# Two matmuls for three in the split-precision products of a two-block network

## The chip, the cores and the metric

The kernel runs on one core of a Trainium2 chip. The time is that of one execution on the device in microseconds (us); of three runs the median is 3662.9 us, the lowest 3659.82 and the highest 3664.96.

## The reference

A sequence of 256 tokens of width 2048 goes through two blocks, in float32. What fills the time is matrix products of the 256 tokens with weights that are read once from memory.

```python
# block 1
mod = silu(c) @ w_ada + b_ada                        # 2048 x 12288, one row
h = modulate(rms_norm(x, norm1_w), shift1, scale1)
p = h @ w_in                                         # 2048 x 4112
x = x + gate1 * (concat(fourier_mix(..), mlstm(..)) @ w_out)      # 2048 x 2048
u = conv3(modulate(rms_norm(x, norm2_w), shift2, scale2) @ w_up)  # 2048 x 11264
a, v = split(u);  x = x + gate2 * ((silu(a) * v) @ w_down)        # 5632 x 2048
x = rms_norm(x, norm_f_w)
# block 2
h = x + 0.5 * rms_norm(swiglu(rms_norm(x)))          # gate and up 2048 x 5632 each, down 5632 x 2048
h = h + rms_norm(mix(rms_norm(h)))                   # S5 scan and sparse attention, ten projections
out = h + 0.5 * rms_norm(swiglu(rms_norm(h)))        # a second feed-forward layer of the same size
```

`mix` projects to the S5 input (1024 columns), keys and values (1536), queries (1024), gates (48), and two sigmoid gates (2048 each); then come a gated unit over the S5 output (1024 x 4096), the attention's output (1024 x 2048) and the last projection (2048 x 2048).

## The kernel before, in words

Everything is held feature-major: a tile has 128 features on the partitions and the 256 tokens along the free dimension (`P` = 128, `T` = 256). A product runs with the weight as the stationary operand, a 128 x 128 tile of it at a time, and the activation tile as the moving one, 256 columns.

Float32 precision comes from a split. Each weight chunk and each activation is written as a high and a low part, float32r tiles of 12 significant bits each, and three of the four cross products are summed: high weight with high activation, low weight with high activation, high weight with low activation. So one pair of a row tile k and a column tile (called a *tile product* below) costs three matmuls of 256 columns, each with a weight load of its own.

`STREAMS` (line 68) lists 21 weight streams with their row tiles and their groups of column tiles. `_tiles` and `_pairs` make groups of four column tiles; "qk_in" has one group of eight and "vg_in" one of four and a narrow one of 16 columns. `lin_steps` (line 317) walks a stream: for every group it takes PSUM banks, two column tiles to a bank, and for every chunk of 1024 weight columns per partition (two row tiles of a four-tile group, so eight tile products) calls `chunk`, then issues the matmuls: for each row tile k, four with the high weight, four with the low one, four with the high one again:

```python
for ci, (a, b) in enumerate(((hi, xh), (lo, xh), (hi, xl))):
    for j in js:
        self.mm(outs[j][0:widths[j]], a[:, c:c + widths[j]], b, ...)
```

`chunk` (line 305) starts the DMA of a raw chunk (SP's queue, four buffers `wr`), copies it to the high part `wh` on ACT (three buffers) and subtracts to get the low part `wl` (two buffers) on DVE, or on POOL for every `pool_every`-th chunk (every chunk of "qk_in" and "vg_in", each second one in the rest of block 1's first part and in the gated unit "glu2" and "gb_in2" of `mix2`, each fifth one at the head of `mix2`, none in the feed-forward layers).

When a group is complete, an evacuation function reads its banks. In the feed-forward layers `ev_up` multiplies or convolves the banks on DVE, applies Silu on ACT, multiplies on POOL and splits the result (`hidden`) into the `hh` and `hl` tiles. `ev_down` takes one column tile at a time, scales it on DVE and squares it on ACT for the next norm's statistics (`add_square`); a stream with `tile_evac` ends its last group tile by tile ("spread"), holding back the last two chunks. `post_norm` then makes the next stage's activations one row tile after the other: two multiplications and an addition on DVE and POOL, a high part on ACT, a low part on DVE.

Eight PSUM banks are one pool `ps` from which the groups and all small products draw. Work that is not on the streams runs as generators in the background: after each chunk `background` advances them by a set share of a step. In the first 500 us that is the modulation `ada_part` (100 MB of `w_ada`, summed on DVE) and the mLSTM and Fourier parts; in the feed-forward layer "up2" it is `s5_tables` (tables computed on POOL); in `mix2` it is the S5 scan (`s5`, on DVE and POOL) and the attention (`nsa`). The order on each engine is fixed when the program is built, by a planner that simulates a timeline (`schedule_with_timeline_sim=True`); a few stretches of DVE are ordered by hand (`manual_schedule` in `post_norm`). Tensors of one tag share a ring of buffers, and an instruction that takes a buffer waits for the last reader of the tile that was in it.

Of the kernel before, what the change touches and what calls it, by code (L numbers as in the profile page):

```python
# [14 lines left out]
P = 128  # L15
T = 256
# [8 lines left out]
# ---------------------------------------------------------------- host layout  # L25
# [6 lines left out]
# Heads are kept as (j, g): head g * 4 + j sits in column block j * 4 + g of the  # L32
# small per-head tables, and pair m holds heads of groups 2 * (m // 4) and the next.
# [18 lines left out]
# A stream is a list of groups; a group is a list of column tiles (index arrays).  # L52
def _tiles(cols, per=4, width=P):
    tiles = [cols[i:i + width] for i in range(0, len(cols), width)]
    return [tiles[i:i + per] for i in range(0, len(tiles), per)]


def _pairs(n_tiles, second):
    out = []
    for i in range(0, n_tiles, 2):  # L60
        out.append([_cols(i * P, P), _cols((i + 1) * P, P),
                    second + _cols(i * P, P), second + _cols((i + 1) * P, P)])
    return out
# [7 lines left out]
    "vg_in": ("w_in", 16, [_tiles(_cols(O_V, 512))[0] + [_cols(O_G, 16)]]),  # L71
# [22 lines left out]
def _chunks(kt, widths):  # L94
    """(first k-tile, k-tiles, offset) of every chunk of a group."""
# [16 lines left out]
def _fm(v):  # L112
    """[n * 128] -> [128, n]"""
    return np.ascontiguousarray(np.asarray(v).reshape(-1, P).T)
# [22 lines left out]
def _constants():  # L137
# [3 lines left out]
    dft = np.stack([c, s]).astype(np.float32)  # [2, 256, 256]  # L141
# [11 lines left out]
    # rows of the gates: forward heads on partitions 0-3, backward heads on 32-35  # L153
# [10 lines left out]
def prepare(inp):  # L164
# [13 lines left out]
    # shift and scale of the first norm, by pair of feature tiles: [pair, eighth of the rows, p, row tile, tile, 2, 128]  # L178
# [31 lines left out]
    for n in ("k", "v"):  # L210
        # rows of two neighbouring block positions fill the partitions: [chunk, (odd, d), pair, 256]
# [12 lines left out]
# ------------------------------------------------------------------- program  # L224


class Builder:
# [12 lines left out]
    # -- tiles  # L240
# [8 lines left out]
    def ring(self, dtype=F32):  # L249
        return self.new(self.p_ring, "r", [P, T], dtype)  # L250
# [7 lines left out]
    def ps(self):  # L258
        return self.new(self.p_ps, "ps", [P, 2, T], F32, 8)
# [5 lines left out]
    # -- short forms  # L265
# [39 lines left out]
    def chunk(self, src, n):  # L305
        """n float32 per partition of a weight: raw -> high and low part"""
# [10 lines left out]
    def lin_steps(self, stream, act, evac=None, tile_evac=None):  # L317
        """Feature-major product: for every group of column tiles, sum over k of
        W[k, tile]^T x[k]. evac(group, banks) gets the group's [128, 2, 256] banks;
        tile_evac(tile, result) gets one column tile, and the last group's tiles then end  # L320
        one after the other. Yields after every chunk of the weight."""
# [4 lines left out]
        for gi, tiles in enumerate(groups):  # L326
# [1360 lines left out]
```

## Time and profile before

| | |
|---|---|
| median of three runs | 3662.9 us (3659.82 to 3664.96) |
| the profiled execution, span from first to last instruction | 3661.0 us |
| PE busy | 3487.1 us, 95% |
| DVE, ACT, POOL busy | 2324.2, 1553.4, 930.1 us |
| read from memory | 694.29 MB, 193 GB/s over the span |
| mean granted clock of TensorE | 0.977 |

The profiled execution has no time of its own beside its span; the span lies between the lowest and the highest of the three runs, 1.9 us under their median. PE is the engine that multiplies, PEld its weight loads, which run beside its matmuls; DVE, ACT and POOL work on tiles, and SP issues the DMAs. A matmul's recorded duration includes its way through the array, which overlaps with the next one: the rate is read from starts, not from durations. A timeline row merges neighbours: its start, its length to the end of its last instruction, and "xN" for how many. The stages by their time in the span: block 1's first part to 500 us, "up1" to 1012, "down1" to 1262, "up2" to 1800, "down2" to 2063, `mix2` to 2862, "up3" to 3390, "down3" to 3643, the last norm to the end.

### The profile page before, as it was taken

To read this page: it belongs to the slowest core of one execution; us is meant where nothing else is said; L and a number is where in the kernel's file an instruction comes from. 1 tells how busy PE (TensorE), PEld (TensorE's weight loads), DVE (VectorE), ACT (ScalarE), POOL (GpSimd) and SP (SyncE) were. 2 spreads that over 40 slices of the span, in tenths; PEclk is the share of its full clock that TensorE was granted. 3 is DMA by queue.
4 is the path that set the end of the run, shared out by engine and by line. 5 is a ranking of instruction groups with operands and counts; after the bars stand their busy time and mean duration, and the time that the engine had idled before them with its cause. 6 is when DMAs were issued, how large, how long until landed. Compare 5 with 4: busy or idle time off the path is not lost.

```text
span 3661.0 us, 67613 instructions
## 1 busy us (share of the span) xinstructions
PE 3487.1 (95%) x27752; PEld 3379.5 (92%) x27752; DVE 2324.2 (63%) x2708; ACT 1553.4 (42%) x1995; POOL 930.1 (25%) x821
## 2 busy tenths in 40 slices
PE   4799999999999997999999899999999899999998
PEld 4688899999999997999999888788899899999997
DVE  8899767776554576555544679886635755555445
ACT  2243355454544443444434432356544544444333
POOL 4443520000011058930000236543232300000001
PEclk8799999999999998999999999999999999999999
DMA  8788857676555564655555455444455455555554
GB/s 298 276 307 300 293 177 230 225 230 203 184 184 182 171 197 160 225 202 184 185 183 182 160 168 175 169 142 125 124 178 182 143 184 184 184 181 183 184 184 139
DMA packets 214327, 710.81 MB, mean 194 GB/s; under 512 B 24016, under 2 KB 39280, under 8 KB 214016
## 3 DMA queue, kind: packets, MB, share of 16 engines
q1 hardware_dynamic: 214016, 706.48, 57.7%
q8 instruction: 217, 3.56, 0.4%
q14 instruction: 94, 0.77, 0.1%
HBM read 694.29 MB, written 11.57 MB: 193 GB/s over the span
## 4 chain that ended last, share of the span: by engine, by line
PE 80%; DVE 8%; POOL 6%; issue 3%; DMA 2%; ACT 1%; SPq 0%; DVEq 0%; POOLq 0%; ACTq 0%
PE ps L295 80%; POOL t L280 3%; DVE t L283 2%; POOL hh L280 1%; DVE wl L277 1%; DVE t L277 1%; DMA wa<-in_w_ada 1%; DMA wr<-in_w_ada 1%; DVE acc L283 1%; DVE w L1393 1%; POOL w L280 1%; POOL wl L280 1%; DVE r L283 0%; POOL acc L280 0%; PE ps L1607 0%
## 5 line engine op out<-in xcount | busy, mean ns | idle before, releaser
L277 DVE TENSOR_TENSOR wl<-wr,wh 128x1024 fp32r<-128x1024 f32 x976 | 1268.2, 1300 | 1076.1 <-PE ps L295 992.5
L274 ACT ACTIVATE wh<-wr 128x1024 fp32r<-128x1024 f32 (+1 forms) x1069 | 1128.3, 1056 | 1672.3 <-PE ps L295 1436.5
L295 PE MATMUL ps<-r,wh 128*128 128x256 f32 x12224 | 1764.6, 287 | 54.0 <-ACT r L274 45.1
L295 PEld LDWEIGHTS ps<-r,wh 128*128 128x128 f32 x12224 | 1605.5, 194 | 65.1 <-ACT r L274 47.5
L295 PE MATMUL ps<-r,wl 128*128 128x256 f32 x6112 | 1005.0, 287 | 47.8 <-DVE wl L277 41.8
L295 PEld LDWEIGHTS ps<-r,wl 128*128 128x128 f32 x6112 | 854.0, 194 | 65.0 <-DVE wl L277 47.8
L280 POOL TENSOR_TENSOR t<-t,t 128x512 f32<-128x512 f32 x66 | 100.6, 1524 | 1299.2 <-ACT t L274 1000.8
L295 PE MATMUL ps<-hh,wl 128*128 128x256 f32 x2112 | 345.0, 283 | 0.0
L295 PE MATMUL ps<-hl,wh 128*128 128x256 f32 x2112 | 345.0, 283 | 0.0
L295 PE MATMUL ps<-hh,wh 128*128 128x256 f32 x2112 | 343.9, 283 | 0.0
L280 POOL TENSOR_TENSOR wl<-wr,wh 128x1024 fp32r<-128x1024 f32 (+1 forms) x93 | 227.5, 2449 | 367.1 <-PE ps L295 245.5
L295 PEld LDWEIGHTS ps<-hh,wl 128*128 128x128 f32 x2112 | 294.0, 192 | 0.0
L295 PEld LDWEIGHTS ps<-hl,wh 128*128 128x128 f32 x2112 | 294.0, 192 | 0.0
L295 PEld LDWEIGHTS ps<-hh,wh 128*128 128x128 f32 x2112 | 293.4, 192 | 0.0
L280 POOL TENSOR_TENSOR acc<-acc,t 128x256 f32<-128x256 f32 x99 | 113.3, 1152 | 597.9 <-ACT t L274 535.6
L283 DVE SCALAR_TENSOR_TENSOR acc<-wr,silu_c,acc 128x1024 f32<-128x1024 f32 x92 | 143.6, 1561 | 37.7 <-DMA wr<-in_w_ada 36.9
L280 POOL TENSOR_TENSOR w<-w,w 128x256 f32<-128x256 f32 x128 | 124.0, 994 | 120.9 <-DVE w L277 102.5
L295 PE MATMUL ps<-m,wh 128*128 128x256 f32 x1024 | 151.2, 285 | 1.0 <-ACT wh L274 1.0
L280 POOL TENSOR_TENSOR t<-hh,hh 128x256 f32<-128x256 f32 (+4 forms) x192 | 145.5, 785 | 2.6
L295 PEld LDWEIGHTS ps<-m,wh 128*128 128x128 f32 x1024 | 133.8, 191 | 4.1 <-ACT wh L274 1.2
L277 DVE TENSOR_TENSOR hl<-t,hh 128x512 fp32r<-128x512 f32 x66 | 63.4, 961 | 50.9 <-ACT hh L274 50.8
L295 PE MATMUL ps<-m,wl 128*128 128x256 f32 x512 | 83.0, 284 | 1.5 <-POOL wl L280 1.5
(233 smaller groups left out, 2220.8 us busy)
## 6 DMA issues: line engine op xcount, KB each, us to landing
wr<-in_w_up SPq DMA_DIRECT2D x528, 512.0 KB, 3.5
wr<-in_w_down SPq DMA_DIRECT2D x264, 512.0 KB, 3.3
wr<-in_w_ada SPq DMA_DIRECT2D x140, 512.0 KB, 4.5
wr<-in_w_out SPq DMA_DIRECT2D x53, 512.0 KB, 4.3
wa<-in_w_ada SPq DMA_DIRECT2D x52, 512.0 KB, 5.0
wr<-in_w_ga_in SPq DMA_DIRECT2D x32, 512.0 KB, 3.3
wr<-in_w_glu SPq DMA_DIRECT2D x32, 512.0 KB, 3.3
wr<-in_w_gb_in SPq DMA_DIRECT2D x32, 512.0 KB, 3.3
```

The lines of the kernel that those rows point to most:

```text
L274: return self.nc.scalar.activation(out=out, in_=in_, func=func, **kw)
L277: return self.nc.vector.tensor_tensor(out, a, b, op=op)
L280: return self.nc.gpsimd.tensor_tensor(out, a, b, op=op)
L283: return self.nc.vector.scalar_tensor_tensor(out=out, in0=a, scalar=s, in1=b, op0=op0, op1=op1)
L295: self.nc.tensor.matmul(out, lhsT, rhs, start=start, stop=stop, skip_group_check=skip)
L1393: nc.vector.tensor_tensor_scan(z[:, k], mg, p[:, k], 0.0, op0=ALU.mult, op1=ALU.add)
```

## The change

The high and low part of an activation become one tile of 2 x 256 columns (`pair`), high first. A tile product is now two matmuls: the high weight with both activation parts in one matmul of 512 columns, which fills one PSUM bank of 512 float32, and the low weight with the high activation part, 256 columns, added into the bank's first half. The second half holds the high weight with the low part, and it is added only when the bank is emptied: `fold` copies the second halves to SBUF on ACT and adds the first halves on DVE. Evacuation then works on the sum in SBUF, where before it read PSUM.

A group is two column tiles, so a chunk holds four row tiles of a group and still eight tile products. Groups have two double banks of their own (`ps2`, tag `pg`), and four single banks `ps` are left for the rest. "qk_in" and "vg_in" keep their three matmuls (`narrow_steps`). Within a row tile the order is now: high weight and low weight of the first column tile, then of the second.

In `ev_down` of the second block's layers the scale by the gain moves from the evacuation to `post_norm`, where it joins the multiplication by `rstd` in one scalar_tensor_tensor; in block 1 the residual takes the two halves in two scalar_tensor_tensor. `hidden` works on single tiles of 256 columns. The rings hold as many bytes as before (25 pairs for 50 tiles, 44 `hh` pairs for 22 + 22). The part of the diff that the prediction speaks of:

```diff
...
-def _tiles(cols, per=4, width=P):
+
+def _tiles(cols, per=2, width=P):
     tiles = [cols[i:i + width] for i in range(0, len(cols), width)]
     return [tiles[i:i + per] for i in range(0, len(tiles), per)]
...
 def _pairs(n_tiles, second):
     out = []
-    for i in range(0, n_tiles, 2):
-        out.append([_cols(i * P, P), _cols((i + 1) * P, P),
-                    second + _cols(i * P, P), second + _cols((i + 1) * P, P)])
+    for i in range(n_tiles):
+        out.append([_cols(i * P, P), second + _cols(i * P, P)])
...
-    def ring(self, dtype=F32):
-        return self.new(self.p_ring, "r", [P, T], dtype)
+    def pair(self):
+
+        return self.new(self.p_ring, "r", [P, 2, T], F32R)
...
-        return self.new(self.p_ps, "ps", [P, 2, T], F32, 8)
+        return self.new(self.p_ps, "ps", [P, 2, T], F32, 4)
+    def ps2(self):
+        return self.new(self.p_ps, "pg", [P, 2, 2, T], F32, 2)
...
+    def fold(self, dst, bank):
+        a, b = bank
+        self.act(dst, b, ACT.Copy)
+        self.tt(dst, a, dst, ALU.add)
+        return dst
...
             if spread:
-                banks = [self.ps() for _ in tiles]
-                outs = [b[:, 0] for b in banks]
+                outs = [self.ps() for _ in tiles]
             else:
-                banks = [self.ps() for _ in range((len(tiles) + 1) // 2)]
-                outs = [banks[j // 2][:, j % 2] for j in range(len(tiles))]
-            starts = [0]
-            for wd in widths:
-                starts.append(starts[-1] + wd)
+                bank = self.ps2()
+                outs = [bank[:, j] for j in range(len(tiles))]
 
             def products(held, js):
                 for hi, lo, k0, kc in held:
                     for k in range(k0, k0 + kc):
-                        xh, xl = act(k)
-                        for ci, (a, b) in enumerate(((hi, xh), (lo, xh), (hi, xl))):
-                            for j in js:
-                                c = (k - k0) * n + starts[j]
-                                self.mm(outs[j][0:widths[j]], a[:, c:c + widths[j]], b,
-                                        start=k == 0 and ci == 0 and (spread or j % 2 == 0),
-                                        stop=k == kt - 1 and ci == 2, skip=True)
+                        x = act(k)
+                        for j in js:
+                            wd = widths[j]
+                            c = (k - k0) * n + j * P
+                            o = outs[j][0:wd]
+                            self.mm(o, hi[:, c:c + wd], x, k == 0, k == kt - 1, True)
+                            self.mm(o[:, 0], lo[:, c:c + wd], x[:, 0], False, k == kt - 1, True)
...
-                evac(gi, banks)
+                evac(gi, bank[:, 0:len(tiles), 0], bank[:, 0:len(tiles), 1])
             else:
                 for j in range(len(tiles)):
                     if spread:
                         products(held, [j])
-                    tile_evac(nt + j, outs[j])
+                    tile_evac(nt + j, outs[j][:, 0], outs[j][:, 1])
...
+    def narrow_steps(self, stream, act, outs, evac):
...
+            for k in range(k0, k0 + kc):
+                x = act(k)
+                for ci, (a, b) in enumerate(((hi, x[:, 0]), (lo, x[:, 0]), (hi, x[:, 1]))):
+                    for j, wd in enumerate(widths):
+                        c = (k - k0) * n + j * P
+                        self.mm(outs[j][0:wd], a[:, c:c + wd], b, k == 0 and ci == 0 and j % 2 == 0,
+                                k == kt - 1 and ci == 2, True)
+            yield
+        evac(outs)
...
-                self.stt(xs[k], res, self.mod[:, 2, k:k + 1], xs[k], ALU.mult, ALU.add)
+                for part in (b, a):
+                    self.stt(xs[k], part, self.mod[:, 2, k:k + 1], xs[k], ALU.mult, ALU.add)
...
-            def ev_up(gi, banks):
-                a = self.t2()
-                v = self.t2()
+            def ev_up(gi, a, b):
+                u, c = self.t2(), self.t2()
+                self.fold(u, (a, b))
                 for j in range(2):
-                    conv(a[:, j], banks[0][:, j], gi * 2 + j)
-                for j in range(2):
-                    conv(v[:, j], banks[1][:, j], KF + gi * 2 + j)
-                s = self.t2()
-                self.act(s, a, ACT.Silu)
-                hid.append(self.hidden(ph, s, v))
+                    conv(c[:, j], u[:, j], gi + j * KF)
+                self.act(c[:, 0], c[:, 0], ACT.Silu)
+                hid.append(self.hidden(ph, c[:, 0], c[:, 1]))
...
-        m = self.t2()
+        m = self.t1()
         self.gtt(m, a, b, ALU.mult)
-        hi = self.new(ph, "hh", [P, 2, T], F32R)
-        lo = self.new(ph, "hl", [P, 2, T], F32R)
-        self.split(m, hi, lo)
-        return hi, lo
+        x = self.new(ph, "hh", [P, 2, T], F32R)
+        self.split(m, x[:, 0], x[:, 1])
+        return x
...
-            def ev_up(gi, banks):
-                g, s, u = self.t2(), self.t2(), self.t2()
-                rb = rstd().unsqueeze(1).to_broadcast([P, 2, T])
-                self.tt(g, banks[0], rb, ALU.mult)
-                self.act(s, g, ACT.Silu)
-                self.tt(u, banks[1], rb, ALU.mult)
-                hid.append(self.hidden(ph, s, u))
+            def ev_up(gi, a, b):
+                g = self.fold(self.t2(), (a, b))
+                self.tt(g, g, rstd().unsqueeze(1).to_broadcast([P, 2, T]), ALU.mult)
+                s = self.t1()
+                self.act(s, g[:, 0], ACT.Silu)
+                hid.append(self.hidden(ph, s, g[:, 1]))
...
-            def ev_down(k, res):
+            fhalf = self.halves(self.p_ring, "r")
+
+            def ev_down(k, a, b):
                 if k == 11:
                     self.warm_sqrt()
-                f = self.ring()
-                self.ts(f, res, gp[:, k:k + 1], None, ALU.mult)
-                self.add_square(st, res)
+                f = self.fold(fhalf(), (a, b))
+                self.add_square(st, f)
                 fs.append(f)
...
-            self.tt(t, fs[k], r, ALU.mult)
+            self.stt(t, fs[k], gp[:, k:k + 1], r, ALU.mult, ALU.mult)
...
+            def scaled(dst, a, b):
+                self.fold(dst, (a, b))
+                self.tt(dst, dst, rb(), ALU.mult)
+                return dst
...
-            def ev_glu(gi, banks):
-                s = self.t2()
-                self.act(s, banks[1], ACT.Sigmoid)
-                self.tt(s, s, banks[0], ALU.mult)
-                for i in range(2):
-                    k = gi * 2 + i
-                    a = sig.pop(("a", k))
-                    self.gtt(a, a, s[:, i], ALU.mult)
-                    ya.append(a)
+            def ev_glu(gi, a, b):
+                f = self.fold(self.t2(), (a, b))
+                s = self.t1()
+                self.act(s, f[:, 1], ACT.Sigmoid)
+                self.tt(s, s, f[:, 0], ALU.mult)
+                y = sig["a", gi // 2][:, gi % 2]
+                self.gtt(y, y, s, ALU.mult)
+                ya.append(y)
...
```

## Rows read from the trace of the kernel before

**Rows 1.** The page's first part: engines over the span.
```profile
PE 3487.1 (95%) x27752; PEld 3379.5 (92%) x27752; DVE 2324.2 (63%) x2708; ACT 1553.4 (42%) x1995; POOL 930.1 (25%) x821
```

**Rows 2.** Windows by stage: length, PE, PEld, DVE, ACT, POOL busy (instructions), clock, DMA.
```profile
180.00:500.00 320.00, 299.89 (x2257) 278.50 (x2256) 256.05 (x251) 133.02 (x218) 134.54 (x73) 0.98 0.81 281
...
1384.00:1600.00 216.00, 197.72 (x1616) 196.26 (x1617) 128.95 (x94) 82.41 (x86) 179.15 (x187) 0.96 0.60 206
...
2098.00:2300.00 202.00, 193.37 (x1415) 170.78 (x1414) 167.08 (x217) 62.21 (x66) 99.80 (x90) 0.98 0.51 171
...
2890.00:3390.00 500.00, 499.92 (x4158) 499.66 (x4159) 275.99 (x247) 211.79 (x225) 35.35 (x28) 1.00 0.55 183
```

**Rows 3.** PE's waits over the span: us in total, times, longest us.
```profile
PE ps L295 <- ACT r L274: 45.1, 13, 7.3
PE ps L295 <- DVE wl L277: 42.7, 24, 14.0
```

**Rows 4.** The groups of matmuls with a low weight part (xcount).
```profile
L295 PE MATMUL ps<-r,wl 128*128 128x256 f32 x6112 | 1005.0, 287 | 47.8 <-DVE wl L277 41.8 <-POOL wl L280 6.0
...
L295 PE MATMUL ps<-hh,wl 128*128 128x256 f32 x2112 | 345.0, 283 | 0.0
...
L295 PE MATMUL ps<-m,wl 128*128 128x256 f32 x512 | 83.0, 284 | 1.5 <-POOL wl L280 1.5
```

**Rows 5.** PE's timeline in "down2": start us, length us, matmuls.
```profile
2000.43 0.64 PE L295 MATMUL ps<-hl,wh 128*128 128x256 f32 x4
2000.91 0.64 PE L295 MATMUL ps<-hh,wh 128*128 128x256 f32 x4
```

**Rows 6.** A window near 53 us, columns as in rows 2.
```profile
52.40:54.20 1.80, 1.80 (x11) 1.80 (x10) 1.80 (x4) 0.28 (x1) 0.08 (x1) 0.50 0.58 202
```

**Rows 7.** PE's timeline in that stretch.
```profile
52.46 1.91 PE L295 MATMUL ps<-r,wl 128*128 128x256 f32 x8
54.17 1.38 PE L295 MATMUL ps<-r,wh 128*128 128x256 f32 x8
```

**Rows 8.** PE's timeline: weights of 48 columns, first and last low-part row.
```profile
2287.79 0.28 PE L295 MATMUL ps<-r,wl 128*48 128x256 f32 x1
...
2292.57 0.28 PE L295 MATMUL ps<-r,wl 128*48 128x256 f32 x1
```

**Rows 9.** PE's timeline: the Fourier product, a new weight for every matmul.
```profile
310.35 0.28 PE L295 MATMUL ps<-dl,m 128*128 128x256 f32 x1
...
310.70 0.28 PE L295 MATMUL ps<-dl,m 128*128 128x256 f32 x1
```

**Rows 10.** Groups of DVE, ACT and POOL by form: busy us, mean ns, idle before.
```profile
L283 DVE SCALAR_TENSOR_TENSOR acc<-wr,silu_c,acc 128x1024 f32<-128x1024 f32 x92 | 143.6, 1561 | 37.7 <-DMA wr<-in_w_ada 36.9
...
L277 DVE TENSOR_TENSOR t<-ps,rstd 128x512 f32<-128x512 f32 x104 | 66.7, 682 | 0.0
...
L283 DVE SCALAR_TENSOR_TENSOR t<-ps,params,t 128x255 f32<-128x255 f32 x176 | 76.6, 476 | 0.6
...
L274 ACT ACTIVATE t<-ps 128x512 f32<-128x512 f32 x20 | 11.5, 603 | 18.6 <-PE ps L295 18.5
...
L280 POOL TENSOR_TENSOR wl<-wr,wh 128x1024 fp32r<-128x1024 f32 x85 | 214.0, 2518 | 367.1 <-PE ps L295 245.5 <-ACT wh L274 95.5 <-ACT w L274 19.7
...
L280 POOL TENSOR_TENSOR t<-hh,hh 128x256 f32<-128x256 f32 x128 | 116.4, 938 | 0.8
```

**Rows 11.** Windows of line 295 on PE at the first groups: length, busy (matmuls), clock.
```profile
500.00:524.00 24.00, 23.63 (x189) 0.96 0.47 157
2867.00:2899.00 32.00, 25.27 (x172) 0.84 0.25 83
```

**Rows 12.** DVE's timeline in "out2", low parts; in brackets idle time before, releaser.
```profile
2828.51 1.22 DVE L277 TENSOR_TENSOR wl<-wr,wh 128x1024 fp32r<-128x1024 f32 x1 [1.66 <-PE ps L295]
```

**Rows 13.** DVE's timeline in `post_norm` before `mix2`.
```profile
2068.73 0.42 DVE L277 TENSOR_TENSOR r<-r,t 128x256 f32<-128x256 f32 x1
...
2072.25 0.95 DVE L277 TENSOR_TENSOR r<-r,t 128x256 f32<-128x256 f32 x1
```

More of the change, by code (lines that the diff above doesn't have):

```diff
@@ L372, in lin_steps @@
                 yield
+    def narrow_steps(self, stream, act, outs, evac):
+        _, kt, (tiles,) = STREAMS[stream]
+        w = self.ap["w_" + stream]
+        widths = [len(t) for t in tiles]
+        n = sum(widths)
+        off = 0
+        outs = outs()
+        for k0, kc in _chunks(kt, widths):
+            size = kc * n
+            hi, lo = self.chunk(w[off:off + P * size].rearrange("(p n) -> p n", p=P), size)
+            off += P * size
+            for k in range(k0, k0 + kc):
[7 more added lines that the diff above has]
+        evac(outs)
     def linear(self, *args, **kw):
@@ L516, in block1 @@
             h = []
-            M = lambda dtype=F32: self.new(pm, "m", [P, T], dtype, 31)
-            res = self.entry(pm, M, xs, h)
+            half = self.halves(pm, "m", 15)
+            pair = lambda: self.new(pm, "m", [P, 2, T], F32R, 15)
+            res = self.entry(pm, half, xs, h)
             def rest():
@@ L606, in entry, with outs_qk, outs_vg, ev_qk @@
         qk, vfm, gates = [], [], []
-        def ev_qk(gi, banks):
+        vbanks = []
+        def outs_qk():
+            banks = [self.ps2() for _ in range(2)]
+            return [banks[j // 4][:, j // 2 % 2, j % 2] for j in range(8)]
+        def outs_vg():
+            vbanks.extend(self.ps() for _ in range(3))
+            return [vbanks[j // 2][:, j % 2] for j in range(5)]
+        def ev_qk(outs):
             for j in range(8):
-                t = M()
-                self.act(t, banks[j // 2][:, j % 2], ACT.Copy, scale=float(np.float32(P ** -0.5)) if j < 4 else 1.0)
+                t = half()
+                self.act(t, outs[j], ACT.Copy, scale=float(np.float32(P ** -0.5)) if j < 4 else 1.0)
                 qk.append(t)
-        def ev_vg(gi, banks):
+        def ev_vg(outs):
             g = self.t1()
@@ L625, in entry @@
         self.pool_every = 1
[L626 removed]
+        streams = self.narrow_steps("qk_in", act_h, outs_qk, ev_qk), self.narrow_steps("vg_in", act_h, outs_vg, ev_vg)
         w = ap["w_ada1"]
@@ L708, in mix1, with ev_v @@
         self.bg.append([ml, 0, 1])
-        def ev_v(gi, banks):
-            for b in banks:
-                fm = self.t2()
-                self.act(fm, b, ACT.Copy)
-                vfm.append(fm)
+        def ev_v(gi, a, b):
+            vfm.append(self.fold(self.t2(), (a, b)))
         dh, dl = new(pm, "dh", [P, 2, 2, T], F32R), new(pm, "dl", [P, 2, 2, T], F32R)
@@ L723, in mix1, with ev_u @@
         uf = []
-        def ev_u(gi, banks):
-            for j in range(4):
-                hi, lo = M(F32R), M(F32R)
-                self.split(banks[j // 2][:, j % 2], hi, lo)
-                uf.append((hi, lo))
+        def ev_u(gi, a, b):
+            f = self.fold(self.t2(), (a, b))
+            for j in range(2):
+                x = pair()
+                self.split(f[:, j], x[:, 0], x[:, 1])
+                uf.append(x)
         self.ada[2] = 2.0
@@ L781, in mix1, with ev_o @@
         yo = []
-        def ev_o(gi, banks):
-            for _ in ml:
-                pass
-            for b in range(2):
-                hd = gi * 2 + b
-                o = self.t2()
-                self.act(o, banks[b], ACT.Sigmoid)
-                self.gtt(o, o, hm[hd], ALU.mult)
-                for i in range(2):
-                    hi, lo = self.ring(F32R), self.ring(F32R)
-                    self.split(o[:, i], hi, lo)
-                    yo.append((hi, lo))
+        def ev_o(gi, a, b):
+            if gi == 0:
+                for _ in ml:
+                    pass
+            o = self.fold(self.t2(), (a, b))
+            self.act(o, o, ACT.Sigmoid)
+            self.gtt(o, o, hm[gi], ALU.mult)
+            for i in range(2):
+                x = self.pair()
+                self.split(o[:, i], x[:, 0], x[:, 1])
+                yo.append(x)
         self.ada[2] = 2.0
```

178 lines of the change are left out of this document (92 added, 86 removed).

## The prediction

> **What bounds the kernel now.** I read the engines' totals first. PE is busy 95% of the span, DVE 63% and ACT 42% [rows 1]. The windows by stage say where such a share is a limit. In "up3" PE is busy in every microsecond at the full clock (1.00), DVE in half of them; in the first 500 us PE has gaps and the DMA engines are at 0.81; from 1384 to 1600 POOL is at 179 of 216 us; at the head of `mix2` DVE is at 167 of 202 us [rows 2]. PE's waits come last: the two longest entries are 45.1 and 42.7 us of a span of 3661 [rows 3]. So outside the first 500 us the matmuls themselves set the time, and what counts is the distance between their starts.
>
> The streams have 6112 + 2112 + 512 = 8736 matmuls with a low weight part, one per tile product [rows 4]. "qk_in" and "vg_in" (16 row tiles of 8 and 5 column tiles, 208) keep their form, so 8528 tile products change. In steady state four matmuls start every 0.48 us, 120 ns each [rows 5], so a tile product costs 360 ns.
>
> **The change, part by part. The matmuls.** Three of 256 columns become one of 512 and one of 256; 768 columns are streamed as before, and one weight load of three goes. What a 512-column matmul takes no row shows. At a granted clock of 0.50 (1.2 GHz) [rows 6], eight matmuls take 1.71 us, 213.5 ns each [rows 7]: 256 columns at one per cycle, with nothing on top. At full clock (2.4 GHz) the columns alone would be 106.7 ns, and 13.3 ns lie above it. So this excess is not a cost per column. With 48-column weights 14 triples take 4.78 us, 113.8 ns per matmul [rows 8]; in the Fourier product, 128-column weights again, a triple takes 0.35 us, 116.7 ns [rows 9]. I read that as some 7 ns for the change of weights and the rest for a weight load that does not quite fit beside 106.7 ns of columns. Beside 512 columns (213.3 ns) it fits with 100 ns to spare; beside the 256 of the low part nothing changes.
>
> The bounds of a pair: below, 213.3 + 2 and 113.8, 329 ns; above, the excess as a share of the columns, 240 + 120 = 360, no gain. A fixed 13.3 ns per matmul gives 226.7 + 120 = 347. I take 216 + 120 = 336 ns, 24 less than now, since the half-clock rows say that the excess disappears where the columns take 213 ns.
>
> The Trainium skill's page "TensorE: Matmul & The Clock Gate" (section "Back-to-back issue gap") gives a warm matmul its columns divided by 2.4 GHz plus 2.5 ns. By it the pair would be 215.8 + 109.2 = 325 ns, an estimate, and the gain 35 ns; the trace has 120 where the rule has 109 for 256 columns, so I use it only as a rival.
>
> Where the gain counts: v, u, o and "out1" (576 tile products) run before 500 us under the load of `w_ada`, so nothing there. The remaining 7952 x 24 ns = 191 us. From it come off:
>
> (a) POOL. From 1384 to 1600 PE issues 1616 matmuls, some 540 tile products, while POOL is 83% busy [rows 2] and a table step costs it six operations of about 1 us [rows 10]; `hidden` now sends it two of 256 columns (about 1 us each) for one of 512. A stretch 7% shorter leaves POOL little room: half the gain, 6 us. (b) While the S5 scan runs DVE is at 83%, shown to 2300 [rows 2], and gets the folds on top. Some 670 tile products (the first four streams of `mix2` and most of the fifth) run beside it: half their gain, 8 us.
>
> (c) First groups. After a norm the row tiles arrive one by one, and the first group can only go as fast as they come. Now that group has four column tiles (64 tile products, 23 us), then two (32, 10.8 us); the second waits behind it in PE's order. Between 2867 and 2899 PE did 172 matmuls, 162 of the stream or 54 tile products, starved [rows 11]; the new group does 32 in that time. 22 x 0.336 = 7.4 us, and the same at the head of `mix2`, which begins with the same `post_norm`. At 500 us the tiles come nearly as fast as they are used (189 matmuls in 24 us) and are complete by 514: 4 us. Together 19 us.
>
> (d) Evacuation and the low part. Each of some 235 groups gains one ACT copy (603 ns) and one DVE addition of 512 columns from PSUM (682 ns) [rows 10]. As busy time that is 140 us on ACT and 160 us on DVE, and both have it: behind PE. But DVE also makes the low parts, in two buffers. Now a chunk's last low-part matmul ends 0.48 us before the chunk does, and the chunk after next needs the new low part 0.48 us into itself: 0.48 + 2.88 + 0.48 = 3.84 us for 1.23 us of work, and DVE idles 1.66 us for PE at each [rows 12]. Then low and high alternate, so the buffer is free at the chunk's end and wanted one matmul into the chunk: 2.69 + 0.22 = 2.91 us. Behind a waiting low part queue the folds, and behind those the bank that the next group but one needs. A feed-forward group of block 2 brings DVE 0.68 + 0.68 + 0.42 = 1.8 us (fold, multiplication, low part of 256 columns [rows 10, 13]); 1.8 + 1.23 = 3.0 us just misses the window. POOL's low part takes 2.52 us [rows 10] and just fits. Bounds: nothing, if the planner puts the two apart, and 230 us (the third rival). I take 28 us, 8 in "up1", which also has the convolutions and `w_ada`'s last part, and 20 in `mix2`, where POOL makes a fifth to a half of the low parts.
>
> (e) Ends of stages. After the last column tile of "out1", three downs and "out2" comes a fold before the square, about 0.8 us each, and the last norm has 16 scalar_tensor_tensor for tensor_tensor: 6 us. The gain moved into `post_norm` is otherwise free, an operation of the same length.
>
> Nothing else moves: the DMAs are the same number and size, SP's queue the same, and the rings hold the same bytes. Sum: 191 - 6 - 8 - 19 - 28 - 6 = 124 us off the profiled 3661, 3537; the median of the runs is 1.9 above that span: 3539, say 3540 us.
>
> **The rivals.** *A fixed cost per matmul.* The 13 ns go with the matmul, whatever its length. For it: narrow weights still leave 7 of them. Against it: none are seen at half clock. Then 7952 x 13.3 = 106 us, less 4 + 4 (a, b) and the same 53 for (c) to (e): 45 us, 3618.
>
> *The leaner pair.* With 35 ns, 278 - 10 - 12 - 53 = 203 us, 3460. For it: 113.8 and 116.7 ns where weights are narrow or the operands are others [rows 8, 9], so the 120 is not a floor; against it: 120 in every steady stretch of the streams.
>
> *The low part comes late; slower.* The change's gain without (d) is 152 us on 7952 / 8 = 994 chunks. If PE waits 0.15 us per chunk, nothing is left. The place is DVE's queue around each evacuation: in "up1" a group's fold, four convolution steps of 0.48 us, low part and a 1.56 us sum of `w_ada` are 4.6 us [rows 10], and with the 1.23 us they are 2.9 over the window, 44 times (128 us); in "up2" and "up3", with DVE's SBUF operations stretched, 0.7 us 88 times (62); in `mix2` 0.2 us on 200 chunks (40). All 230 us would give 3661 - 152 + 230 = 3739; nearer to what half-mixed queues do, 3710. For it: the window shrinks by a quarter. Against it: DVE has a third of its time free, the same bursts exist now without a wait in "up3", and the planner spreads them. DVE's additions of two SBUF operands take 0.95 us beside POOL and 0.42 without [rows 13]. The Trainium skill's page "SBUF — State Buffer" (section "Who interferes with whom") says that a DVE instruction with two SBUF inputs contends with a POOL instruction that reads SBUF; the trace agrees, and the change turns PSUM inputs into such ones. It speaks for this rival.
>
> *The change does not do what it says*: 512 columns pass like two of 256, 240 ns, and a pair is 360. Then only losses stay, (c), (e) and some of (d): 45 us, 3708. Against it speak the half-clock rows.
>
> **How the numbers follow.** Forecast 0.52, with its own range 3500 to 3580; fixed cost 0.19; leaner pair 0.11; late low part 0.12; no gain per pair 0.06. The range reaches over the first three: 3455 to 3655. About 0.2% (7 us) can be told from no change. Faster by more: 0.52 + 0.19 + 0.11, of which 0.02 of the second falls short, and 0.02 of the late low parts are mild: 0.82. Within it: 0.04. Slower: 0.14.
>
> **What would show it.** In "down2" the starts of a pair: 336 ns for the forecast (216 and 120), 347, 325, or 360. The waits: PE on DVE `wl` under 80 us in all, or hundreds. In the windows, "down1" and "down3" about 7% shorter, "up3" 6%, the first 500 us as long as now. At 2000 to 2100 the first group of `mix2` starving as long as now, for half the work. The forecast is wrong if the pair is at 345 or more, or if PE waits for low parts or for banks by more than 60 us over what it does now.

## The result: slower by 1.5%, and the profile after

Median 3716.6 us (3712.6 to 3718.5) against 3663.9: ratio 1.0146, 95% interval 1.013 to 1.0162. The profiled execution has a span of 3713.9 us, 3661.0 before. The forecast was 3540 us. PE is at 93% instead of 95%; DVE and ACT took on the copies and additions, as forecast. The page's first part, after (compare [rows 1]):

```profile
PE 3454.7 (93%) x19224; PEld 2923.0 (79%) x19224; DVE 2432.9 (66%) x2989; ACT 1707.6 (46%) x2381; POOL 938.1 (25%) x887
```

PE's busy time fell by 32 us (3487.1 to 3454.7), and its idle time, the rest of the span, rose by 85 us (173.9 to 259.2). The mean granted clock fell from 0.977 to 0.966.

First the pair, the two matmuls of a tile product, in "down2", where nothing waits. Groups of matmuls from 1880 to 2040 us, by form (count, busy us, mean ns of one), after and then before:

```profile
L318 PE MATMUL pg<-hh,wh 128*128 128x512 f32 x459 | 160.1, 395 | 0.0
L318 PE MATMUL pg<-hh,wl 128*128 128x256 f32 x459 | 127.0, 279 | 0.0
```

```profile
L295 PE MATMUL ps<-hh,wh 128*128 128x256 f32 x446 | 71.8, 283 | 0.0
```

160 us over 459 pairs is 349 ns a pair. The mean ns of one (395 and 279) is no price: neighbours overlap in the records. In the same stretch before, 446 triples take 160 us, 359 ns. So a tile product became 10 ns cheaper, not 24.

The 349 is a mean of two prices. Six pairs lie between the first and the last row of each of these two stretches of PE's timeline in "down2":

```profile
1925.29 0.40 PE L318 MATMUL pg<-hh,wh 128*128 128x512 f32 x1
...
1927.41 0.40 PE L318 MATMUL pg<-hh,wh 128*128 128x512 f32 x1
```

```profile
1960.26 0.39 PE L318 MATMUL pg<-hh,wh 128*128 128x512 f32 x1
...
1962.34 0.39 PE L318 MATMUL pg<-hh,wh 128*128 128x512 f32 x1
```

That is 353 ns a pair and 347. In the three downs the groups go at these two prices in turn; in "up3" nearly all steady chunks go at 353.

Then PE's waits over the span (us in total, times, longest us), to be compared with [rows 3]:

```profile
PE pg L318 <- DVE wl L293: 81.7, 64, 5.8
...
PE pg L318 <- ACT r L290: 29.6, 8, 7.3
PE pg L318 <- DVE r L299: 27.8, 5, 6.8
...
PE pg L318 <- ACT wh L290: 12.7, 12, 4.9
```

The wait for low parts (`wl`) went from 24 times to 64. Most of the new ones sit in "up1", after and before:

```profile
PE pg L318 <- DVE wl L293: 18.1, 26, 1.4
```

```profile
PE ps L295 <- DVE wl L277: 0.4, 1, 0.4
```

One of them, in DVE's timeline (start us, length us, in brackets the idle time before and its releaser):

```profile
642.13 1.23 DVE L293 TENSOR_TENSOR wl<-wr,wh 128x1024 fp32r<-128x1024 f32 x1 [0.95 <-PE pg L318]
645.24 1.28 DVE L299 SCALAR_TENSOR_TENSOR acc<-wr,silu_c,acc 128x1024 f32<-128x1024 f32 x1 [1.88 <-DMA wr<-in_w_ada]
646.44 0.68 DVE L293 TENSOR_TENSOR t<-pg,t 128x512 f32<-128x512 f32 x1
647.04 1.22 DVE L293 TENSOR_TENSOR wl<-wr,wh 128x1024 fp32r<-128x1024 f32 x1
```

and on PE:

```profile
648.31 0.39 PE L318 MATMUL pg<-r,wl 128*128 128x256 f32 x1 [0.56 <-DVE wl L293]
```

DVE stands at the sum of `w_ada` until its transfer lands, then comes the fold, then the low part, and PE has been waiting for 0.56 us. The stage lengths, each from the end of the stage before it to its own last low-part matmul (from the starts of those matmuls; us), with four of the experiments told below:

```
            before  after  twolast  wl3t  lolast  lobf4v
to out1      492.1  511.2   492.4  502.5   498.6   497.7
up1          518.8  534.1   531.1  511.2   508.2   506.2
down1        253.8  255.3   257.7  254.6   254.3   251.5
up2          544.1  550.5   545.5  540.5   548.8   524.0
down2        253.8  250.2   256.0  250.3   249.4   249.6
mix2         797.6  817.4   812.5  803.1   806.7   802.4
up3          526.4  521.9   530.3  520.6   516.5   512.9
down3        253.8  251.8   256.0  254.4   250.9   247.9
```

Only up3, down2 and down3 got shorter; the first 500 us, up1, up2 and mix2 lost 61 us.

Idle time is not all of the loss. Summed over the stretches in which the trace shows a granted clock of 0.50, PE was busy for 160 us at that half clock, against 100 before. In `mix2` it was 48 us against 23, with 47 us idle against 25; in "up1", whose waits are short (18.1 us in 26 times), only 6 against 3. A pair takes 640 ns at half clock and 347 at full clock (run m3 below), so the 60 us more cost some 27 us, an estimate. Since busy time fell by 32 us all the same, the cheaper pairs gave back some 60 us over the whole program, not the 80 that 10 ns on 7952 tile products would be.

### The profile page after: what moved, and what is told of

It is laid out like the page before. It is cut to its first block, busy times and chain, and to the rows that moved or that the text cites. A ratio compares the mean times of both kernels' runs of the same rounds, so it can differ in the third digit from the quotient of the medians.

```text
span 3713.9 us, 51218 instructions
## 1 busy us (share of the span) xinstructions
PE 3454.7 (93%) x19224; PEld 2923.0 (79%) x19224; DVE 2432.9 (66%) x2989; ACT 1707.6 (46%) x2381; POOL 938.1 (25%) x887
## 5 line engine op out<-in xcount | busy, mean ns | idle before, releaser
L318 PE MATMUL pg<-r,wh 128*128 128x512 f32 (+1 forms) x6112 | 2146.4, 400 | 72.9 <-ACT r L290 29.6
L318 PE MATMUL pg<-r,wl 128*128 128x256 f32 x5984 | 1677.7, 288 | 85.8 <-DVE wl L293 79.7
L318 PEld LDWEIGHTS pg<-r,wh 128*128 128x128 f32 x6112 | 1150.6, 193 | 335.3 <-ACT r L290 30.3
L318 PEld LDWEIGHTS pg<-r,wl 128*128 128x128 f32 x5984 | 1147.3, 193 | 139.2 <-DVE wl L293 105.3
L318 PE MATMUL pg<-hh,wh 128*128 128x512 f32 x1848 | 646.5, 396 | 0.0
L318 PE MATMUL pg<-hh,wl 128*128 128x256 f32 x1848 | 513.3, 279 | 0.0
L318 PEld LDWEIGHTS pg<-hh,wh 128*128 128x128 f32 x1848 | 345.7, 188 | 81.8
L318 PEld LDWEIGHTS pg<-hh,wl 128*128 128x128 f32 x1848 | 348.2, 188 | 1.7
L318 PE MATMUL pg<-m,wh 128*128 128x512 f32 x496 | 180.1, 402 | 0.0
L318 PE MATMUL pg<-m,wl 128*128 128x256 f32 x496 | 141.5, 285 | 2.1 <-DVE wl L293 2.0
```

The costliest lines, as they stand in the source:

```text
L318: self.nc.tensor.matmul(out, lhsT, rhs, start=start, stop=stop, skip_group_check=skip)
```

## Experiments

Two questions: what a 512-column matmul costs, and where the rest is lost. The theory for the loss is late low parts (DVE's shorter window). Its rivals are the grouping by two and the second halves with their additions; for the pair, the forecast's reading of the excess stands against a fixed cost. Ratios are against the kernel before.

**m1: matmuls alone.** The core of it, shortened, with `cols`, weights and formats changed from block to block:

```
for i in range(256):
    mm(o, wt(i)[128 x 128], x[i // 2 % 4][:, 0:cols], i == 0, i == 255)
```

> A kernel of matmul blocks alone, 256 matmuls each on one bank, all operands in SBUF beforehand: 256 columns with new weights each time (one), 512 columns (two), 512 and 256 in turn (pair), the same with one set of weights (onesame, twosame), 48-column weights (narrow), two-byte operands (bfone, bftwo), 128 and 384 columns (quarter, threeq), and 256 and 512 again while the weight pipeline (load, ACT copy, DVE subtraction of 128x1024) runs beside them (lone, ltwo). If the excess over 106.7 ns is one per matmul or a weight load that does not fit (the reading behind the forecast): one 118 to 120 ns, two 214 to 220, quarter about 66 or held at about 118 by the load, pair 334 to 340, onesame and narrow below one by 5 ns or more. If a column itself takes longer than half a 1.2 GHz cycle: one 117 to 120, two 232 to 240, threeq about 176, quarter about 60, pair 350 to 360, weights the same or narrow change little. If other traffic on SBUF makes the excess: one at 109 to 113 and two at 216 to 220, lone and ltwo 4 per cent longer.

Groups of m1 (of the first 256-column block, "one", six matmuls were issued at the very start, some 213 ns apart; the later ones have none of these):

```profile
L21 PE MATMUL pair<-xh,wh 128*128 128x512 f32 (+1 forms) x512 | 90.6, 340 | 0.0
...
L21 PE MATMUL twosame<-xh,wh 128*128 128x512 f32 x256 | 58.2, 389 | 0.0
L21 PE MATMUL ltwo<-xh,wh 128*128 128x512 f32 x256 | 58.2, 389 | 0.0
L21 PE MATMUL bftwo<-xb,wb 128*128 128x512 bf16 x256 | 55.4, 379 | 0.0
...
L21 PE MATMUL threeq<-xh,wh 128*128 128x384 f32 (+1 forms) x257 | 44.8, 334 | 0.0
...
L21 PE MATMUL lone<-xh,wh 128*128 128x256 f32 x256 | 30.9, 283 | 0.0
L21 PE MATMUL onesame<-xh,wh 128*128 128x256 f32 x256 | 30.9, 283 | 0.0
...
L21 PE MATMUL narrow<-xh,wh 128*48 128x256 f32 (+1 forms) x257 | 30.4, 280 | 0.0
L21 PE MATMUL quarter<-xh,wh 128*128 128x128 f32 (+1 forms) x257 | 29.1, 275 | 0.0
L21 PE MATMUL bfone<-xb,wb 128*128 128x256 bf16 x256 | 28.1, 273 | 0.0
```

From start to start within a block: 120.0 ns for 256 columns, 173.3 for 384, 226.7 for 512. Less the columns at 2.4 GHz (106.7, 160, 213.3) that leaves 13.3 each time: a fixed cost for each matmul of four-byte operands. The same weights every time (onesame, twosame; a weight load is still issued for each matmul) and the weight pipeline running beside (lone, ltwo) change nothing. Two-byte operands carry 2.5 (109.2 and 215.8). The Trainium skill's page "TensorE: Matmul & The Clock Gate" (section "Back-to-back issue gap") gives an isolated matmul at full clock its columns over 2.4 GHz plus 2.5 ns: the two-byte blocks agree, the four-byte ones don't. A 128-column matmul takes 112 ns, far over 53 + 13: something else sets the pace there, and what it is stays open. And the pair, in turn on one bank, takes 353.3 ns, 6.6 more than 120.0 + 226.7.

**m3: the same at half clock.** Bursts behind 18 us of rest, shortened:

```
for _ in range(20): vector.tensor_scalar(dl, dl, 1.0, mult)   # TensorE rests
scalar.activation(x, dl, Copy)                                # the burst waits for x
for i in range(n): mm(o[i % 2], wt(i), x, False, i >= n - 2)
```

> Bursts of matmuls behind some 15 to 20 us in which TensorE rests, so that each burst begins at the half clock: 64 of 256 columns (cone), 32 of 512 (ctwo), 24 pairs of 512 and 256 on two banks in turn (cpair), 64 two-byte ones of 256 (cbf), thrice; then 256 each of the first three (wone, wtwo, wpair), whose later part runs at full clock. The forecast took 213.5 ns for 256 columns at half clock as proof that the excess over the columns vanishes in time that is there; the blocks at full clock have 226.8 for 512, 13.5 over the columns. If the excess belongs to the full clock: at half clock 512 columns take 427, a pair 640 to 641, two-byte matmuls 213 to 214, and at full clock 120.0, 226.8 and 347 again. If the excess comes per matmul at both and 213.5 was a chance of few records: 440, 225 or more for 256, a pair 665.

A burst of 512 columns in m3, timeline rows (six matmuls lie between their starts), then windows (length, PE busy, granted clock):

```profile
414.10 3.62 PE L21 MATMUL wtwo<-x,wh 128*128 128x512 f32 x8
...
416.66 1.05 PE L21 MATMUL wtwo<-x,wh 128*128 128x512 f32 x2
```

```profile
414.00:417.00 3.00, 3.00 (x8) 0.50 0.00 0
418.00:470.00 52.00, 52.00 (x230) 1.00 0.00 1
```

2.56 us / 6 = 427 ns at a clock of 0.50: the columns alone, nothing on top. At 1.00: 52 us / 230 = 226 ns. From half to full clock, pairs go from 640 ns (427 and 213) to 347, 256 columns from 213 to 120, two-byte ones from 213 to 109. So the half-clock row behind the forecast was read rightly, but it says nothing of the full clock: the 13.3 ns belong to the full clock, and they came with every length measured there from 256 columns up, also where the columns take 213 ns. Why is open.

**m2: the order in a pair.** The high part's and low part's products in runs of one or eight, on one bank or two, with a four-byte or two-byte low part (shortened):

```
for s in range(0, 256, run):
    for i in range(s, s + run): mm(big(i), wt(i), x[i // 2 % 4], False, ...)
    for i in range(s, s + run): mm(low(i), wl(i), x[i // 2 % 4][:, 0], False, ...)
```

> Blocks of matmuls alone again, 256 products each with a 512-column high part and a 256-column low part, weights new each time: in turn (turn), eight high then eight low (eight), in turn with the products on two banks alternately (turnb), in turn with the low part in a bank of its own (apart), the low part with two-byte weights and activations (turnbf in turn, eightbf in eights, eightbfb in eights on two banks), and two-byte 256-column matmuls alone whose activations are every second two-byte element (stride). From the first blocks (120.0 and 226.8 ns alone, 353.3 ns in turn) the taking of turns costs 6.5 ns: eight should be 347 to 348, turn and turnb 353. If that extra is the low part adding to columns just written, apart is 347; if it is the change of length, apart is 353. Two-byte low parts took 109 ns alone: eightbf 336 to 337, if every second element is read as fast as every one; stride then 109, else 120 or more.

Groups of m2, three that hold both members of the pair:

```profile
L21 PE MATMUL turn<-xh,wh 128*128 128x512 f32 (+1 forms) x514 | 92.6, 342 | 0.0
L21 PE MATMUL eight<-xh,wh 128*128 128x512 f32 (+1 forms) x514 | 90.0, 337 | 0.0
L21 PE MATMUL turnb<-xh,wh 128*128 128x512 f32 (+1 forms) x514 | 89.4, 336 | 0.0
```

Per pair: turn 353.3, eight 349.2, turnb and apart 346.7. In these blocks all of the extra goes when products alternate between two banks, and a part of it with runs of eight. The expectation that turnb would be 353 failed. The bank is not the whole of it: the changed kernel alternates its banks, as turnb, and still half of its groups in "down2" go at 353; what sets them apart is open. Two-byte matmuls of 256 columns that read every second element take 113.3 ns alone (block stride), so a pair with a two-byte low part would be 340 ns from its parts. It took 362.2 in turn and 346.7 in eights, not the 336 expected: a change of format has a price of its own, which with the 4 ns for every second element eats the 10.8 ns. Why is open.

**split: fusing alone.**

```
-  self.mm(o, hi[:, c:c + wd], x, k == 0, k == kt - 1, True)
+  self.mm(o[:, 0], hi[:, c:c + wd], x[:, 0], k == 0, k == kt - 1, True)
+  self.mm(o[:, 1], hi[:, c:c + wd], x[:, 1], False, k == kt - 1, True)
```

> The changed kernel with its 512-column matmul issued as two of 256 columns into the same two halves; groups of two, halves, copies and additions all stay. This is the price of fusing alone. If the fusion saves 24 ns per tile product (forecast), 8528 of them give 200 us more than the changed kernel, about 3920 us, and the rest of the change costs 255 us. If 512 columns take twice the time of 256 and only some 8 ns go, it takes 60 to 70 us more, 3775 to 3790. If fusing saves nothing at all and only fills waits, it is within 15 us of the changed kernel, 3717.

3754.0 us, ratio 1.0242 (1.022 to 1.0264): 37 us more than the changed kernel. Fusing is a gain: in "down2" split takes 360 ns a tile product, the changed kernel 349. The 37 us lie between the expected cases; the 200 us of the forecast's reading are excluded.

**two256: without halves and additions.** Split, with `x[:, 1]` also into `o[:, 0]`, and

```
-  self.act(dst, b, ACT.Copy)
-  self.tt(dst, a, dst, ALU.add)
+  self.act(dst, a, ACT.Copy)
```

> The changed kernel with three 256-column matmuls, all into the first half of a bank, the DVE addition left out (the copy reads the one half; after out1 and down1 one scalar_tensor_tensor instead of two). What stays of the change is the groups of two column tiles with low and high products in turn. Against split it gives the price of the second halves and their additions; against the kernel before that of the grouping. If the additions in DVE's queue make the low parts late: 60 to 90 us under split, at 3690 to 3720. If the grouping is the loss (first groups after a norm, shorter window for the low part): within 25 us of split, 3760 to 3790. By the prediction's own terms (c and the grouping's share of d 30 us): about 3695.

3737.1 us, 1.0203 (1.0181 to 1.0225): the halves and additions cost some 17 us (the two intervals just touch), not the 60 to 90 expected if they were the loss, and 72 us of loss are left with neither fusing nor halves.

**twolast: the same, low parts last.** As lolast below, on two256.

> two256 (groups of two, three 256-column matmuls into one half, no addition) with a chunk's sixteen high-weight products first and its eight low-part products last. It parts the 72 us by which two256 is over the kernel before. If they are the late low parts (high and low in turn leave DVE 2.9 us per chunk): 45 to 65 us faster than two256, 3675 to 3692. If they are the grouping (the first groups after a norm, more copies): within 20 us of two256, 3720 to 3740. The prediction's (c) alone leaves 19 us over the kernel before, 3684.

3709.1 us, 1.0122 (1.0105 to 1.0139): 28 us of the 72 were the order. 45 to 65 were expected if it was late low parts alone, so half of that holds; some 44 us stay with the groups of two.

**lolast: low parts last in the chunk.**

```
+  for part in range(2):
     for hi, lo, k0, kc in held: ...
-        self.mm(o, hi, x, ...); self.mm(o[:, 0], lo, x[:, 0], ...)
+        if part == 0: self.mm(o, hi, x, ...)
+        else: self.mm(o[:, 0], lo, x[:, 0], ...)
```

> The changed kernel with a chunk's eight 512-column products first and its eight low-part products behind them; matmuls, DMAs, copies, additions the same. A new low part is then wanted some 1.9 us into its chunk instead of 0.23, with the buffer free at the same chunk end: the window of DVE for it grows from 2.9 to 4.7 us. If PE's 82 us of waits for wl are the loss: 45 to 70 us faster than the changed kernel, 3650 to 3670. If the loss is DVE's or PE's work itself or the grouping, within 15 us of it, 3700 to 3732.

3654.6 us, 0.9978 (0.9965 to 0.9991): 62 us under the changed kernel with the same instructions, and slightly faster than before.

**wl3t: a third buffer instead of another order.**

```
-  NB = (4, 3, 2)
+  NB = (4, 3, 3)        # and t1 6 -> 4, t2 5 -> 4 to make room
```

> The changed kernel in its own order, with a third buffer for low parts (paid with two buffers less of 256 and one less of 512 columns among DVE's and ACT's temporaries). The low part of a chunk may then be made a whole chunk (2.8 us) earlier. If late low parts are the loss that the other order gave back: 40 to 65 us faster than the changed kernel, 3650 to 3677, with PE's waits for wl down from 82 to under 40 us. If that gain came from the order in PE itself (no taking of turns), or the fewer temporaries cost as much: within 15 us, 3700 to 3730.

3661.3 us, 0.999 (0.9978 to 1.0001): 55 us under the changed kernel by another way to the same end. PE's waits for `wl`, lolast and wl3t:

```profile
PE pg L318 <- DVE wl L293: 33.2, 26, 4.5
```

```profile
PE pg L318 <- DVE wl L293: 35.1, 30, 3.9
```

In "up1", DVE's idle time ahead of the `w_ada` sums (the last figures of a row, us) in the kernel before, in the changed kernel and in wl3t (lolast has 30.8):

```profile
L283 DVE SCALAR_TENSOR_TENSOR acc<-wr,silu_c,acc 128x1024 f32<-128x1024 f32 x30 | 38.5, 1285 | 23.3 <-DMA wr<-in_w_ada 23.2
```

```profile
L299 DVE SCALAR_TENSOR_TENSOR acc<-wr,silu_c,acc 128x1024 f32<-128x1024 f32 x30 | 38.5, 1285 | 56.5 <-DMA wr<-in_w_ada 56.5
```

```profile
L299 DVE SCALAR_TENSOR_TENSOR acc<-wr,silu_c,acc 128x1024 f32<-128x1024 f32 x30 | 38.6, 1285 | 33.3 <-DMA wr<-in_w_ada 33.3
```

So late low parts probably fed themselves there. The raw ring `wr` is freed by the low part, the next load of `w_ada` waits for the ring, DVE for that load, and the next low part behind DVE. That chain is argued from the order in the queue; the runs show its two ends.

**beflast: that order on the kernel before.** Products in the order hi·xh, hi·xl, lo·xh over the whole chunk.

> The kernel before (groups of four column tiles, three 256-column matmuls, no halves) with only the order in a chunk changed: all high-weight products first, the low-part products last. If lateness of the low part is worth 43 us there too (PE's wait for wl before), 20 to 40 us faster than before, 3625 to 3645, and then fusing has no merit of its own against it. If the kernel before has little of it to lose since its low parts were in the middle: 3655 to 3670, and lolast's lead over it is the fusion's.

3679.5 us, 1.0038 (1.0023 to 1.0053): 13 us slower, a miss of both expected cases. PE's waits for `wl` stayed as they were (45.0 us against 42.7), so the order took no lateness away there. At the head of `mix2` the first 64 tile products took 46.7 us against 42.6: after a norm a chunk's high products want all its row tiles first, which is argued and covers only a part of the 13. At equal order the grouping by two costs 30 us (twolast less beflast), the fusing with its halves gives back 55 (lolast).

**lobf, lobf4, lobf4v: a version faster than both.** lolast with the low part in two-byte floats; then four buffers for it (the products of the compressed keys take two-byte low parts too, so that they fit); then the hidden tile's multiplication on DVE in "up2". The low-part products are no longer the same arithmetic: a two-byte float keeps fewer bits of the low weight and of the activation beside it. Shortened:

```
-  lo = self.new(self.p_w, "wl", [P, CH], F32R, self.NB[2])
+  lo = self.new(self.p_w, "wl", [P, CH], BF16, self.NB[2])
-  self.mm(o[:, 0], lo[:, c:c + wd], x[:, 0], ...)
+  self.mm(o[:, 0], lo[:, c:c + wd], x[:, 0].bitcast(BF16)[:, 1::2], ...)
-  NB = (4, 3, 2)                      # lobf4
+  NB = (4, 3, 4)
-  self.gtt(m, a, b, ALU.mult)         # lobf4v, in hidden
+  (self.tt if self.hd else self.gtt)(m, a, b, ALU.mult)
```

> lolast with the low weight part kept in two-byte floats, its matmul reading the upper two bytes of the high activation part where it lies; nothing else is new (DVE writes the low part with half the bytes). If a matmul of four-byte operands carries 13.3 ns above its columns and one of two-byte operands 2.5 (the blocks: 120.0 against 109.2 ns at 256 columns), each of 8736 low-part matmuls gets 10.8 ns shorter: 94 us at most, 70 to 85 where PE sets the time, 3570 to 3585. If the excess is a matter of columns or of other traffic on SBUF, or every second element costs a second pass, it is at lolast's 3655 or above.

> lobf with four buffers for the two-byte low parts instead of two, in the same room (the compressed keys' products use two-byte low parts too, that they fit). PE still waits 37.6 us for wl in lobf. If these are late DVE subtractions that more buffers let run ahead: 15 to 30 us faster than lobf, 3595 to 3610. If DVE is then simply late for its other work (folds, row tiles after a norm): within 10 us, 3615 to 3635.

> lobf4 with the multiplication that makes a hidden tile moved from POOL to DVE in up2 alone, where POOL is busy 58 of 60 us while it makes the tables of the S5 scan. If POOL is what holds the hidden tiles, the banks behind them or the tables there (the prediction's a): up2 10 to 20 us shorter, 3580 to 3600. If DVE is the one that is late in up2: no gain or up to 15 us longer.

lobf 3624.4 us, 0.9886 (0.9867 to 0.9904), short of the 70 to 85 us expected: the chunks' period gives a pair of 347 ns, 2.5 less than in lolast (349.1) and the same as in m2. lobf4 3628.4, 0.9912 (0.9891 to 0.9933), no gain, though PE's waits for `wl` fell from 37.6 to 5.5 us: those for ACT's `wh` rose from 16.1 to 27.6, for its `r` from 32.4 to 36.8. A wait removed went to the next in line. lobf4v 3615.3, 0.9872 (0.9854 to 0.989), is the lowest median, clear of lobf4's runs, while its interval overlaps that of lobf: "up2" is 13 us shorter than in lobf4. Windows from 1400 to 1600 us of lobf4 and lobf4v (PE, PEld, DVE, ACT, POOL busy):

```profile
1400.00:1600.00 200.00, 182.79 (x1013) 136.34 (x1012) 130.21 (x115) 85.09 (x116) 185.85 (x191) 0.97 0.62 209
```

```profile
1400.00:1600.00 200.00, 190.50 (x1071) 142.92 (x1070) 154.28 (x140) 91.73 (x122) 173.00 (x170) 0.98 0.64 220
```

So in lobf4 POOL held PE there; DVE, with 24 us more to do, did not.

## Why the prediction was wrong

The forecast was 177 us too low (3716.6 less 3540). In its own steps:

**The pair is the step that failed**: "the half-clock rows say that the excess disappears where the columns take 213 ns". It does at half clock (427 ns for 512 columns) and does not at full clock (226.7). Measured were 349 ns for 336, a gain of 10 ns for 24; the forecast's own sign of being wrong, a pair at 345 or more, came true. At 10 ns the 7952 tile products would give 80 us for 191; PE's busy time shows some 60 (an estimate, above), since much of the program went at 353. That is 131 of the 177. The rival of a fixed cost per matmul (347, chance 0.19) had the mechanism; its argument against, that none is seen at half clock, is what fell. "Some 7 ns for the change of weights" was wrong too: with the same weights a matmul takes 120.0 as well. With narrow weights 117.2 stay in m1. The two prices of a pair, 347 and 353, were in no part of the prediction.

**The losses** were forecast at 67 us. With the gain of 60 and the 53 by which the kernel ended slower they come to 113, 46 us more: 85 us of idle time and the 27 us at half clock make up nearly all of it. The prediction has no term for the clock. The parts below overlap, so they are not a sum.

(d) Evacuation and low part: 28 forecast, "8 in up1". Two different ways of making the low parts less urgent give 55 and 62 us (wl3t and lolast). The places were only half right: forecast were 8 us in up1 and 20 in `mix2`; wl3t and lolast give back 23 and 26 in up1, 14 and 11 in `mix2`, 9 and 12 in the first 500 us. The shorter window, and DVE's queue around each evacuation with the `w_ada` sum in it, fit what was found. The size was not right: the sum was counted as 1.56 us of work (it took 1.29 in up1), but DVE also stands idle ahead of it for its load, 1.88 us in the rows above. The slower rival (0.12) named that place, and its price for "up1" alone, 128 us, was five times too high.

(c) First groups: 19 forecast. From the end of the stage before to the 64th tile product, up1 went from 31.4 to 34.3 us, u_in2 from 42.6 to 48.4, up3 from 42.6 to 48.0. That is 14 us of the 19: the step holds. The window at the head of up3 (columns as in [rows 2]; [rows 11] has 172 matmuls and a clock of 0.84 there) shows the starving, and the clock with it at 0.68:

```profile
2919.00:2951.00 32.00, 14.69 (x54) 11.35 (x55) 29.21 (x39) 15.97 (x36) 20.10 (x22) 0.68 0.14 48
```

(a) POOL in up2: 6 forecast. Up2 lost 20 (6.4 longer, and the 14 that 10 ns a pair would be, not seen); low parts are in that too, 26.8 us of waits. lobf4v shows 13 us of POOL's, in lobf4 and not in the changed kernel itself. The cause was right; its size was about twice the forecast, if it is the same there.

The first 500 us were to stay as they are and got 19 us longer: with low parts last they take 498.6 (lolast), with a third buffer 502.5 (wl3t), so about half of it or more is late low parts there too. The prediction took no gain from these 500 us ("so nothing there") and looked for no loss in them: this term was missing.

(b) and (e) were not tested by themselves. With "fusing" the prediction also took for granted that nothing else in the pair would matter; m2 shows 0 to 6.6 ns for where and in which order the products are accumulated.

## What to carry to other kernels

A cost read at one clock, or in one length, is not carried to another: measure the new form by itself first, in a block of some hundred instructions at the clock where it will run. When an order of products changes, count for each double-buffered operand from its last use to its next need, and put what else is in the producer's queue into that window, the waits of those operations too and not only their busy time. Where PE starves for long, read the granted clock of that stretch too: here its half clock cost some 27 us beside 85 us of idle time. If the window is short, put the products that need the late operand last: that was worth 62 us here without an instruction more.

## What the runs showed of the hardware

At full clock a matmul of four-byte operands took its columns at 2.4 GHz and 13.3 ns, at 256, 384 and 512 columns; one of two-byte operands its columns and 2.5 ns (109.2 and 215.8 at 256 and 512); at half clock they took the columns alone (four-byte 213 and 427 ns at 256 and 512 columns, two-byte 213 at 256). 128 columns took 112 ns. In blocks alone a pair of four-byte 512 and 256 columns cost 6.6 ns more when all pairs accumulate into one bank than on two in turn (353.3 and 346.7); in the changed kernel, on two banks in turn, both prices occur. Four-byte 512 and two-byte 256 columns in turn cost 362 ns a pair, in eights 347, where the parts alone are 340. Reading every second two-byte element cost 113.3 ns for 256 columns, against 109.2. The weight pipeline on DMA, ACT and DVE beside a block changed nothing that can be seen (120.0 and 226.7 ns with and without).
